# State space tables moved behind the modulation, its small operations moved to ScalarE, in the first stage of a two-block kernel

## The chip, the cores and the metric

One core of a Trainium2 chip. The metric is the device time of one execution in microseconds; the median of three runs stands for the kernel. Five engines work side by side: TensorE (PE, with its weight loads PEld), VectorE (DVE), ScalarE (ACT), GpSimd (POOL) and SyncE (SP), which issues most of the DMAs.

## The reference, cut to what matters

Two blocks are computed on 512 tokens of width 1024. Only the beginning of the first one matters here: the condition `c` gives shift, scale and gate through `w_ada`; the input is normed, scaled and shifted; then it is projected. Beside that, the state space mixer needs tables that hang on the weights alone: `lam_bar`, its powers, and `b_bar`.

```python
def first_block(x, c, ...):
    cond = jax.nn.silu(c)
    mod = cond @ w_ada[l] + b_ada[l]
    shift, scale, gate = jnp.split(mod, 3, axis=-1)
    h = rms_norm(x, norm_g[l]) * (1.0 + scale[:, None, :]) + shift[:, None, :]
    proj = h @ w_in[l]
    ssm_u, ssm_z, q, k, v, attn_z, q_idx, k_idx, w_idx = jnp.split(proj, split_points, axis=-1)
    y_ssm = s5_mixer(ssm_u, a_re[l], a_im[l], log_dt[l], b_re[l], b_im[l], ...)
    y_attn = dsa_mixer(q, k, v, q_idx, k_idx, w_idx, ...)
    ...

def s5_mixer(u, a_re, a_im, log_dt, b_re, b_im, ...):
    lam = lax.complex(a_re, a_im)
    dt = jnp.exp(log_dt)[:, None]
    lam_bar = jnp.exp(lam * dt)
    b_bar = ((lam_bar - 1.0) / lam)[..., None] * (b_re + i b_im)
    ...

def dsa_mixer(...):
    rel = jnp.einsum('bqhd,bsd->bqhs', qib, k_idx)       # the indexer
    score = jnp.einsum('bqh,bqhs->bqs', wib, jax.nn.relu(rel))
    _, sel = lax.top_k(score, topk)
    ...
```

## The kernel before, in words

The kernel holds the activations transposed: 8 tiles of 128 channels by 512 tokens. A product in full precision is made of three products of hi and lo parts (`mm3`, L152 to L155): `split` (L142 to L146) lets ScalarE round a tile to its hi part and VectorE or GpSimd subtract it to get the lo part.

**The modulation** (`block1`, from L448). For each tile k the rows of `w_ada` for shift and scale are loaded (`fetch`, L473) and multiplied with the condition `cB`. `weigh` (L486 to L492) does this on VectorE, where one instruction also sums (L490), or on GpSimd (L492), where ScalarE sums afterwards (`total`, L496). Shifts are weighed on VectorE, scales of the tiles 1 to 6 on GpSimd. `modulate(k, R)` (L498 to L504) then adds `b_ada` (L500) and forms (1 + scale) * norm_g (L501), both operations on one or two columns; L502 multiplies xT with it and with the row of inverse norms R, which lies in PSUM; L503 (ScalarE) adds the shift and rounds to the hi part hTh; L504 (VectorE) makes the lo part hTl. Of each tile `u_part(k)` takes 12 products for the state space input, and `i_part(k)` three for the indexer's keys. GpSimd makes the lo parts of their weights (`split_u`, `split_i`, L146).

**The tables** (`ssm_tables`, from L1106). This is a generator. Its first part, up to `yield None` (L1172), makes the exponential and sine and cosine of `lam * dt`, the powers of `lam_bar` (PW), and the factors kr and ki; nearly all are VectorE operations on 128 x 16 elements, one per `yield` (96 in all; the helpers are `poly_exp`, `sincos` with L1043 to L1057, `cmul` with L1065 and L1067). The second part makes Bb and the products BP (q 0 and 1 on VectorE, 2 and 3 on GpSimd), and then GpSimd makes the table of rotations `turn`, which starts from the phase and rho products L1194 to L1200.

In `block1` `step(n)` draws n steps of the first part. 40 are drawn at the beginning, 20 behind the making of the diagonal for R, and 8 after each `modulate(k)`, so that the first part is done after tile 4. Those 56 steps hold 59 VectorE instructions.

**The order of the work.** TensorE, SyncE and, in the first stage, ScalarE execute in the order of the program. The order on VectorE and GpSimd is fixed by the compiler's scheduler, by the order of the program and by what it takes to be ready; `tc.issue_after(x)` keeps the VectorE instructions of a block behind instruction x. All engines execute in the order that results.

**Behind it** the second part of the tables is drawn by `weave` (L230) together with the indexer's product:

```python
tables = later(tables)      # each step issued after `last`, the last hTl
self.weave(self.both(self.bias_table(), self.alongside(ssm_chunks(), tables)), indexer())
```

`weave` draws from `main` and lets each step's cost (the number that it yields, 0.12 for a small table operation, 0.62 for a product BP) buy steps of `indexer()`, 0.49 for three products of 384 columns. The indexer takes four column blocks; each ends with two evictions by `stack` (ScalarE L891, VectorE L892), out of two PSUM buffers. Its weights are loaded in four pieces and split by ScalarE (L145) and VectorE (L146). Then the scores (`index_scores`, L947 to L954) and the selection (`top_mask`, L965 to L974) follow, woven with the state space scan and with projections, and then attention.

Of the kernel before, what the change touches and what calls it, by code (L numbers as in the profile page):

```python
# [8 lines left out]
F32 = mybir.dt.float32  # L9
F32R = mybir.dt.float32r  # L10
I32 = mybir.dt.int32
AF = mybir.ActivationFunctionType
OP = mybir.AluOpType
# [91 lines left out]
class Kern:  # L105
# [342 lines left out]
    def block1(self):  # L448
        nc, A, tc = self.nc, self.A, self.tc
        sm = self.sm  # L450
        TT, TS, STT = nc.vector.tensor_tensor, nc.vector.tensor_scalar, nc.vector.scalar_tensor_tensor
# [16 lines left out]
        def fetch(k):  # L468
            wts[k] = []
            for v in range(2):  # L470
                tag = ("wlo", "whi")[v]
                wts[k].append(self.wp.tile([128, 1024], F32, name="wada", tag=tag, bufs=self.wbufs[tag]))
                nc.sync.dma_start(wts[k][v], wada[v * D + k * 128:v * D + (k + 1) * 128])  # L473
# [4 lines left out]
        def fetch_u(k):  # L478
            raw[k] = self.pg("uraw")
            nc.sync.dma_start(raw[k], A["w_in"][k * 128:(k + 1) * 128, 0:512])  # L480
            wu[k] = uhi[:, k], self.sp.tile([128, 512], F32R, name="ulo", tag=f"F{'ri'[k // 4]}{k % 4}", bufs=1)

        def split_u(k, eng):
            self.split(raw[k], *wu[k], eng=eng)

        def weigh(k, v, eng):  # L486

            w, m = wts[k][v], mod[:, 2 * k + v:2 * k + v + 1]
            if eng is nc.vector:
                eng.tensor_tensor_reduce(out=w, in0=w, in1=cB, scale=1.0, scalar=0.0, op0=OP.mult, op1=OP.add, accum_out=m)  # L490
            else:
                eng.tensor_tensor(out=w, in0=w, in1=cB, op=OP.mult)  # L492

        def total(k, v):
            w = wts[k][v]
            nc.scalar.activation(w, w, AF.Identity, accum_out=mod[:, 2 * k + v:2 * k + v + 1])  # L496

        def modulate(k, R):  # L498
            m = mod[:, 2 * k:2 * k + 2]
            TT(out=m, in0=m, in1=self.col("b_ada")[:, k:k + 9:8], op=OP.add)  # L500
            STT(out=m[:, 1:2], in0=m[:, 1:2], scalar=1.0, in1=self.col("norm_g", k), op0=OP.add, op1=OP.mult)  # L501
            STT(out=xT[k], in0=xT[k], scalar=m[:, 1:2], in1=R, op0=OP.mult, op1=OP.mult)  # L502
            nc.scalar.activation(hT[0][k], xT[k], AF.Identity, bias=m[:, 0:1])  # L503
            return STT(out=hT[1][k], in0=xT[k], scalar=m[:, 0:1], in1=hT[0][k], op0=OP.add, op1=OP.subtract)  # L504

        tables = self.ssm_tables()

        ready = []

        def step(n):  # L510
            while n and not ready:
                n -= 1
                if next(tables) is None:
                    ready.append(True)

        uacc = []

        def u_part(k):
            for j in range(4):
                if k == 0:  # L520
                    uacc.append(self.ps((128, 512), "ggss"[j]))
                self.mm3(uacc[j], [w[:, j * 128:(j + 1) * 128] for w in wu[k]], [v[k] for v in hT], k == 0, k == 7)
# [5 lines left out]
        def fetch_i():  # L528
            for h in range(2):
                iraw.append(self.pg("iraw").rearrange("p (k n) -> p k n", n=128)[:, :, :72])  # L530
                nc.sync.dma_start(iraw[h], A["w_in"][h * 512:(h + 1) * 512, 3584:3656].rearrange("(k p) n -> p k n", p=128))

        def split_i():
            for h in range(2):
                v = [self.pg("iw", F32R).rearrange("p (k n) -> p k n", n=128)[:, :, :72] for _ in range(2)]
                self.split(iraw[h], *v, eng=P)
                wk.extend([(v[0][:, k], v[1][:, k]) for k in range(4)])

        def i_part(k):
            self.mm3(kacc, wk[k], [v[k] for v in hT], k == 0, k == 7)  # L540

        with tc.manual_schedule(engines={mybir.EngineType.Activation}):
            V, P = nc.vector, nc.gpsimd
            for k in range(8):
                nc.sync.dma_start(xT[k], A["xT"][k * 128:(k + 1) * 128])
                if k == 7:
                    nc.sync.dma_start(cB, A["c_row"])
                self.square(xT[k], acc[k % 2], k // 2, (P if k % 2 else V) if k < 6 else (V if k == 7 else P))
            nc.scalar.activation(cB, cB, AF.Silu)
            step(40)  # L550
            for k in range(4):
                fetch(k)
                fetch_u(k)
                if k == 1:
                    fetch_i()
            warm = self.sm.tile([128, 1], F32, name="warm", tag="warm", bufs=1)
            nc.scalar.activation(warm, self.ones[:, 0:1], AF.Sqrt)
            TT(out=acc[0], in0=acc[0], in1=acc[1], op=OP.add)
            r = self.stats(acc[0])
            weigh(0, 0, V)  # L560
            weigh(0, 1, V)
            split_u(0, P)
            R = self.rows(r,'psum')
            with tc.issue_after(self.diag.ins):
                weigh(1, 0, V)
                step(20)
            weigh(1, 1, P)
            for k in range(8):
                last = modulate(k, R)
                with tc.issue_after(last.ins):  # L570
                    step(8)
                if 0 < k + 1 <= 6:
                    total(k + 1, 1)
                if k < 6:
                    weigh(k + 2, 1, P if k + 2 <= 6 else V)
                if k < 7:
                    split_u(k + 1, P)
                if k < 6:
                    weigh(k + 2, 0, V)
                if k == 0:  # L580
                    split_i()
                u_part(k)
                if k >= 0:
                    i_part(k - 0)
                if k < 4:
                    fetch(k + 4)
                    fetch_u(k + 4)
                    if k + 4 == 1:
                        fetch_i()
            for k in range(8, 8):  # L590
                i_part(k)
            with tc.issue_after(last.ins):
                step(1000)
            self.ssm_loads()
            self.ssm_inputs()
        self.dump("hT", hT[0])
# [17 lines left out]
        def later(stream):  # L614

            while True:
                with tc.issue_after(last.ins):
                    ask = next(stream, None)
                if ask is None:
                    return  # L620
                yield ask

        tables = later(tables)
# [482 lines left out]
    def ssm_tables(self):  # L1106
        nc, A, big = self.nc, self.A, self.sp
        TT, TS, STT = nc.vector.tensor_tensor, nc.vector.tensor_scalar, nc.vector.scalar_tensor_tensor
# [9 lines left out]
        def norm():  # L1118
            TT(out=den, in0=ar, in1=ar, op=OP.mult)
            yield 0.12  # L1120
            TT(out=t1, in0=ai, in1=ai, op=OP.mult)
            yield 0.12
            TT(out=den, in0=den, in1=t1, op=OP.add)
            yield 0.12
            nc.vector.reciprocal(den, den)
            yield 0.12

        dt, _ = yield from self.abreast(self.poly_exp(lam[:, 32:48], 16, "dt"), norm())
# [40 lines left out]
        yield from self.abreast(powers(PW, 7), coef())  # L1169
        self.PW = PW  # L1170

        yield None  # L1172
        B = self.Bm
        Bb = self.two("Bb")
        tb = self.two("tb") + self.two("tb")
# [32 lines left out]
        n = 1  # L1208
# [658 lines left out]
```

## Time and profile before

| | |
|---|---|
| median of three runs | 1264.85 us (1262.48 to 1265.42) |
| the profiled execution: time, span | 1264.23 us, 1262.2 us |
| mean granted TensorE clock | 0.973 |
| PE busy | 1161.3 us, 92% of the span |
| DVE busy | 823.2 us, 65% |
| ACT busy | 548.1 us, 43% |
| POOL busy | 450.0 us, 36% |

Times in the trace are counted from the start of the span. Busy time holds waiting too: an instruction that has started and waits for a port of the memory is shown as running. Small instructions overlap, so that several of 0.17 us can start 0.08 us apart. A wait in brackets is idle time of the engine before an instruction, with what ended it.

### The profile page before, as it was taken

The numbers are of one execution on the slowest core, as the hardware profiler recorded it, in microseconds if no ns is written. First come the engines' busy times: TensorE is split into PE (matmuls) and PEld (weight loads), VectorE is DVE, ScalarE is ACT, GpSimd is POOL, SyncE is SP. The second block draws the span as 40 slices with busy tenths as digits, with TensorE's granted clock in tenths as the row PEclk, the third lists the DMA queues.
The fourth block names the chain that finished last, engine by engine and source line by source line (L and its number), as shares of the span: only waits on it lengthen the run. The fifth ranks groups of instructions, "written<-read, shape, count | busy, mean of one in ns | idle before, by whom it ended". The sixth has DMA issues, their size and how long they took to land.

```text
span 1262.2 us, 17119 instructions
## 1 busy us (share of the span) xinstructions
PE 1161.3 (92%) x6264; PEld 949.0 (75%) x6264; DVE 823.2 (65%) x1602; ACT 548.1 (43%) x1022; POOL 450.0 (36%) x546
## 2 busy tenths in 40 slices
PE   2667888977899999898999999999999999999998
PEld 2457787965678998886777777688888888888876
DVE  7986999438765466786767575564577743577731
ACT  4333532145663543555565555433444421344420
POOL 4679689048532037245666565201000000000000
PEclk9797988988999999999999999999999999999999
DMA  9452113145134442232111111134333233333330
GB/s 355 140 151 69 35 54 103 34 151 166 34 103 159 149 121 61 68 101 67 35 34 51 34 34 35 50 100 150 101 94 90 90 98 96 100 92 92 98 111 34
DMA packets 112755, 118.05 MB, mean 94 GB/s; under 512 B 16184, under 2 KB 101216, under 8 KB 112672
## 3 DMA queue, kind: packets, MB, share of 16 engines
q1 hardware_dynamic: 102432, 107.20, 26.9%
q10 hardware_dynamic: 10240, 9.77, 2.4%
q8 instruction: 49, 0.80, 0.3%
q14 instruction: 34, 0.28, 0.1%
HBM read 109.47 MB, written 6.30 MB: 92 GB/s over the span
## 4 chain that ended last, share of the span: by engine, by line
PE 76%; DVE 17%; ACT 2%; issue 2%; DMA 1%; POOL 1%; ACTq 0%; DVEq 0%; POOLq 0%
PE ps_g L153 20%; PE ps_g L154 20%; PE ps_g L155 19%; PE ps_t L369 4%; PE ps_o L383 4%; DVE wlo L146 2%; PE ps_s L342 2%; PE ps_s L341 2%; DVE score L954 1%; PE ps_t L1321 1%; DVE score L971 1%; DVE wada L490 1%; DVE m L970 1%; PE ps_o L1659 1%; PE ps_t L1325 1%
## 5 line engine op out<-in xcount | busy, mean ns | idle before, releaser
L145 ACT CAST whi<-wraw 128x1024 fp32r<-128x1024 f32 (+4 forms) x161 | 161.8, 1011 | 170.1 <-PE ps_g L154 136.6
L146 DVE TENSOR_TENSOR wlo<-wraw,whi 128x1024 fp32r<-128x1024 f32 (+4 forms) x143 | 174.8, 1228 | 69.4 <-ACT whi L145 69.3
L153 PE MATMUL ps_g<-hT,whi 128*128 128x512 f32 x504 | 206.6, 410 | 0.0
L155 PE MATMUL ps_g<-hT,wlo 128*128 128x512 f32 x504 | 197.9, 393 | 0.0
L154 PE MATMUL ps_g<-hT,whi 128*128 128x512 f32 x504 | 196.3, 390 | 0.0
L350 POOL TENSOR_TENSOR P<-P,rsum 128x256 f32<-128x256 f32 (+3 forms) x144 | 100.4, 727 | 76.2 <-DVE rsum L1446 34.3
L345 ACT ACTIVATE P<-P,nm 128x128 f32<-128x128 f32 (+3 forms) x160 | 89.7, 561 | 85.4 <-DVE nm L343 84.7
L153 PEld LDWEIGHTS ps_g<-hT,whi 128*128 128x128 f32 x504 | 95.1, 189 | 24.4 <-issue 9.3
L155 PEld LDWEIGHTS ps_g<-hT,wlo 128*128 128x128 f32 x504 | 94.7, 188 | 21.9
L154 PEld LDWEIGHTS ps_g<-hT,whi 128*128 128x128 f32 x504 | 95.0, 189 | 17.9 <-issue 1.2
L343 DVE CUSTOM_DVE_ANT_0 P<-ps_s,att 128x128 f32<-128x128 f32 (+3 forms) x128 | 62.1, 485 | 50.6 <-PE ps_t L369 29.4
L369 PE MATMUL ps_t<-consts,P 128*128 128x128 f32 x400 | 66.3, 279 | 11.4 <-DVE qst L895 7.5
L153 PE MATMUL ps_g<-act,whi 128*128 128x512 f32 (+1 forms) x176 | 70.8, 403 | 0.0
L155 PE MATMUL ps_g<-act,wlo 128*128 128x512 f32 (+1 forms) x176 | 68.8, 391 | 0.0
L154 PE MATMUL ps_g<-act,whi 128*128 128x512 f32 (+1 forms) x176 | 68.8, 391 | 0.0
L153 PE MATMUL ps_g<-whi,hTh 128*128 128x256 f32 x192 | 61.2, 319 | 7.0 <-ACT sq L666 4.3
L369 PEld LDWEIGHTS ps_t<-consts,P 128*128 128x128 f32 x400 | 46.7, 141 | 26.9 <-issue 14.7
L855 POOL TENSOR_TENSOR acc<-acc,sq 128x512 f32<-128x512 f32 x15 | 21.9, 1461 | 117.9 <-ACT sq L854 115.2
L153 PE MATMUL ps_g<-whi,hT 128*128 128x256 f32 (+1 forms) x208 | 59.0, 284 | 2.8 <-ACT sq L1361 2.8
L154 PE MATMUL ps_g<-wlo,hT 128*128 128x256 f32 (+1 forms) x208 | 58.5, 281 | 2.4 <-DVE wlo L146 2.4
L155 PE MATMUL ps_g<-whi,hT 128*128 128x256 f32 (+1 forms) x208 | 58.4, 281 | 0.0
L154 PE MATMUL ps_g<-wlo,hTh 128*128 128x256 f32 x192 | 56.4, 294 | 0.9 <-DVE wlo L146 0.9
(508 smaller groups left out, 2915.8 us busy)
## 6 DMA issues: line engine op xcount, KB each, us to landing
wraw<-in_w_in_dram SPq DMA_DIRECT2D x56, 512.0 KB, 3.4
wraw<-in_w_up_dram SPq DMA_DIRECT2D x40, 512.0 KB, 3.7
wada<-in_w_ada_dram SPq DMA_DIRECT2D x16, 512.0 KB, 7.2
wraw<-in_w_down_dram SPq DMA_DIRECT2D x16, 512.0 KB, 3.4
wadag<-in_w_ada_dram SPq DMA_DIRECT2D x8, 512.0 KB, 4.5
wraw<-in_w_out_dram SPq DMA_DIRECT2D x8, 512.0 KB, 3.3
wraw<-in_w_attn_br_dram SPq DMA_DIRECT2D x8, 512.0 KB, 3.4
wraw<-in_w_o_dram SPq DMA_DIRECT2D x8, 512.0 KB, 3.4
```

Source lines behind the costliest of these rows:

```text
L145: nc.scalar.copy(hi, src)
L146: (eng or nc.vector).tensor_tensor(out=lo, in0=src, in1=hi, op=OP.subtract)
L153: mm(out, lhsT=l[0], rhs=r[0], start=start, stop=False)
L154: mm(out, lhsT=l[0], rhs=r[1], start=False, stop=False)
L155: mm(out, lhsT=l[1], rhs=r[0], start=False, stop=stop)
L341: nc.tensor.matmul(s, lhsT=q, rhs=khi[:, :w], start=True, stop=False)
L342: nc.tensor.matmul(s, lhsT=q, rhs=klo[:, :w], start=False, stop=True)
L343: nc.vector.tensor_tensor_reduce(out=P[i], in0=s, in1=madd(i), scale=-1.0, scalar=3.0e38, op0=OP.add, op1=OP.min, accum_out=nm[:, i:i + 1])
L345: nc.scalar.activation(P[i], P[i], AF.Exp, scale=-1.0, bias=nm[:, i:i + 1], accum_out=sums[:, i:i + 1])
L350: nc.gpsimd.tensor_tensor(out=P[n], in0=P[n], in1=sc[:, n:n + 1].to_broadcast([128, (n + 1) * 128]), op=OP.mult)
L369: nc.tensor.transpose(pt[:, o:o + 128], P[i][:, j * 128:(j + 1) * 128], self.ident)
L383: nc.tensor.matmul(acc[x * 64:(x + 1) * 64, j * 128:], lhsT=V(j), rhs=tiles[b][:, o:o + w], start=start and j == 0, stop=stop and j == 2)
```

## The change

The first part of the tables is no longer drawn between the modulations. The 40 steps at the beginning stay; the rest is drawn by the weave with the indexer's product, where the second part already stands, and so behind the last hTl. The `yield None` that parted the two is gone. In `modulate` the two small VectorE operations become two ScalarE operations: the shift gets its bias by an Identity with a column of `b_ada` as bias, and the scale by one with `norm_g` as scale and a column of the new table `one` = (b_ada + 1) * norm_g as bias, which one VectorE operation makes at the start for all eight tiles.

```diff
         def modulate(k, R):
             m = mod[:, 2 * k:2 * k + 2]
-            TT(out=m, in0=m, in1=self.col("b_ada")[:, k:k + 9:8], op=OP.add)
-            STT(out=m[:, 1:2], in0=m[:, 1:2], scalar=1.0, in1=self.col("norm_g", k), op0=OP.add, op1=OP.mult)
+            nc.scalar.activation(m[:, 0:1], m[:, 0:1], AF.Identity, bias=self.col("b_ada", k))
+            nc.scalar.activation(m[:, 1:2], m[:, 1:2], AF.Identity, scale=self.col("norm_g", k), bias=one[:, k:k + 1])
             STT(out=xT[k], in0=xT[k], scalar=m[:, 1:2], in1=R, op0=OP.mult, op1=OP.mult)
...
+        one = self.cp.tile([128, 8], F32, name="one")
+        STT(out=one, in0=self.col("b_ada")[:, 8:16], scalar=1.0, in1=self.col("norm_g"), op0=OP.add, op1=OP.mult)
         tables = self.ssm_tables()
 
-        ready = []
-
         def step(n):
-            while n and not ready:
-                n -= 1
-                if next(tables) is None:
-                    ready.append(True)
+            for _ in range(n):
+                next(tables)
...
             with tc.issue_after(self.diag.ins):
                 weigh(1, 0, V)
-                step(20)
             weigh(1, 1, P)
             for k in range(8):
                 last = modulate(k, R)
-                with tc.issue_after(last.ins):
-                    step(8)
                 if 0 < k + 1 <= 6:
                     total(k + 1, 1)
...
-            with tc.issue_after(last.ins):
-                step(1000)
             self.ssm_loads()
             self.ssm_inputs()
...
         yield from self.abreast(powers(PW, 7), coef())
         self.PW = PW
 
-        yield None
         B = self.Bm
```

## Rows read from the trace of the kernel before

**Rows 1.** Busy time by stretch: stretch and its length, then each engine, clock, DMA.
```profile
24.65:69.91 45.26, 31.87 (x101) 21.88 (x100) 44.47 (x106) 16.15 (x29) 29.01 (x34) 0.85 0.44 152
69.91:109.70 39.79, 25.50 (x128) 22.44 (x126) 30.08 (x33) 12.48 (x23) 32.10 (x54) 0.87 0.40 120
109.70:185.00 75.30, 64.79 (x557) 61.66 (x558) 66.03 (x116) 33.26 (x67) 59.24 (x64) 0.87 0.18 57
185.00:1262.20 1077.20, 1035.72 (x5469) 839.61 (x5468) 664.58 (x1285) 475.36 (x889) 321.42 (x386) 0.99 0.28 87
```

**Rows 2.** Waits from 15 to 76 us: who waits for whom, total, times, longest.
```profile
ACT hTh L503 <- DVE xT L502: 34.0, 7, 7.8
```

**Rows 3.** Timeline, 0 to 40 us: start, duration, engine, line, operation, tiles.
```profile
34.06 3.75 DVE L1055 SCALAR_TENSOR_TENSOR trc<-trc,tr 128x16 f32<-128x16 f32 x3
34.17 2.34 POOL L492 TENSOR_TENSOR wada<-wada,cB 128x1024 f32<-128x1024 f32 x1
...
36.52 1.26 POOL L146 TENSOR_TENSOR ulo<-uraw,uhi 128x512 fp32r<-128x512 f32 x1
```

**Rows 4.** The tile mod, 0 to 70 us: shortest, median and longest in ns.
```profile
L500 DVE TENSOR_TENSOR mod<-mod,vecs x8: 146/178/1246, 18.8 to 65.6; 128x2 f32<-128x2 f32 x8
L501 DVE SCALAR_TENSOR_TENSOR mod<-mod,vecs x8: 145/156/2261, 19.9 to 65.8; 128x1 f32<-128x1 f32 x8
```

**Rows 5.** Chain of waits, 0 to 180 us: start, the time it takes there, what.
```profile
57.07 1.14 DVE wada L490
58.21 0.67 DVE hTl L504
```

**Rows 6.** Timeline: first tile's modulation, and hTh of tile 6.
```profile
24.65 0.17 DVE L1000 SCALAR_TENSOR_TENSOR erq<-erq,err 128x16 f32<-128x16 f32 x1
...
25.38 0.74 DVE L502 SCALAR_TENSOR_TENSOR xT<-xT,mod,ps_t 128x512 f32<-128x512 f32 x1
...
26.15 0.72 ACT L503 ACTIVATE hTh<-xT,mod 128x512 fp32r<-128x512 f32 x1 [7.76 <-DVE xT L502]
...
66.70 0.72 ACT L503 ACTIVATE hTh<-xT,mod 128x512 fp32r<-128x512 f32 x1 [2.82 <-DVE xT L502]
```

**Rows 7.** GpSimd's groups, 18.7 to 69.9 us: busy us, mean ns, idle before.
```profile
L146 POOL TENSOR_TENSOR iw<-iraw,iw 128x288 fp32r<-128x288 f32 x2 | 1.6, 794 | 0.0
...
L1195 POOL TENSOR_TENSOR kt<-trs 128x16 f32<-128x16 f32 x1 | 0.2, 211 | 0.0
```

**Rows 8.** Timeline, 0 to 40 us, ScalarE.
```profile
17.68 0.21 ACT L278 ACTIVATE rt<-ms 128x4 f32<-128x4 f32 x1 [3.36 <-DVE ms L277]
...
34.80 1.04 ACT L496 ACTIVATE wada<-wada 128x1024 f32<-128x1024 f32 x1
...
35.84 0.60 ACT L145 CAST uhi<-uraw 128x512 fp32r<-128x512 f32 x1
```

**Rows 9.** Timeline, 68 to 130 us, VectorE.
```profile
68.59 1.32 DVE L504 SCALAR_TENSOR_TENSOR hTl<-xT,mod,hTh 128x512 fp32r<-128x512 f32 x1 [0.38 <-ACT hTh L503]
...
75.11 1.73 DVE L146 TENSOR_TENSOR wlo<-wraw,whi 128x1024 fp32r<-128x1024 f32 x1 [4.68 <-ACT whi L145]
...
83.51 0.68 DVE L1065 TENSOR_TENSOR t<-kpwr,Bb 128x512 f32<-128x512 f32 x1
...
92.07 0.55 DVE L892 TENSOR_TENSOR iq<-ps_g,iq 64x384 fp32r<-64x384 f32 x1
...
109.13 0.56 DVE L892 TENSOR_TENSOR iq<-ps_g,iq 64x384 fp32r<-64x384 f32 x1 [0.54 <-ACT iq L891]
```

**Rows 10.** Timeline, 68 to 190 us, GpSimd and TensorE.
```profile
70.24 1.79 POOL L1103 COPY CD<-ssm 64x256 f32<-64x256 f32 x4
...
97.46 0.66 PE L153 MATMUL ps_g<-hTh,whi 128*128 128x384 f32 x1 [11.97 <-DVE iq L892]
...
142.80 1.28 POOL L1288 TENSOR_TENSOR rot<-turn,E 128x512 f32<-128x512 f32 x1 [8.44 <-issue]
```

**Rows 11.** VectorE's groups, 18.7 to 69.9 us: busy us, mean ns, idle before.
```profile
L1055 DVE SCALAR_TENSOR_TENSOR trc<-trc,tr 128x16 f32<-128x16 f32 x7 | 6.6, 937 | 0.1
```

## The prediction, made before the change was run

> **What bounds the kernel now.** The change touches the first 110 us, so I read the trace there in stretches, from the engines' busy shares down to single instructions. The busy table by stretch [rows 1] shows four regimes. In the first stage (24.65 to 69.91, modulation and first products) VectorE is busy 44.47 of 45.26 us and TensorE 31.87. In the second (to 109.70, the indexer's product beside the state space tables) no engine is full, yet something is always waited for. In the third (to 185) VectorE is busy 66.03 of 75.30. Behind 185 TensorE is busy 96% and the work is fixed. So the end of the kernel moves by as much as the first two stages give, if the third passes it on.
>
> The waits of the first stage [rows 2] name one thing: ScalarE's hi cast of a tile (hTh, L503) waits seven times, 34.0 us together, for VectorE's scaling of xT (L502). What holds VectorE is seen in the timeline [rows 3]: three operations on 16 elements (L1055) take 3.75 us, and end when GpSimd's weighing product (34.17 to 36.51) and lo part (36.52 to 37.78) end. An operation with two inputs in SBUF waits out GpSimd's instruction; L502, with its second input in PSUM, never does. The two small modulation operations (L500, L501) take 0.15 us alone and up to 1.25 and 2.26 [rows 4]. So the full VectorE is mostly a VectorE that waits for GpSimd, and the stage is bound by what the two may not do at once.
>
> **The sum.** Per tile that exclusive work is GpSimd's lo part 1.26 and weighing 2.34 [rows 3], VectorE's weighing 1.14 and hTl 0.67 [rows 5]: 5.4 us. Measured from the hTh of tile 0 to that of tile 6 [rows 6] it is (66.70 - 26.15) / 6 = 6.76. The rest is what the change takes away:
> - Tables: 59 VectorE instructions leave the stage. Free, they start 0.08 apart (24.65 to 25.38 holds nine of them) [rows 6], I take 0.088: 5.2 us. With them go 18 small GpSimd products on their results (phase and rho, L1194 to L1200), 0.21 each [rows 7]: 3.8.
> - Modulation: 16 small VectorE operations, 0.15 each [rows 4]: 2.4.
>
> That is 11.4 us of exclusive time, but not all is path. Worked forward: L502 of tile 0 starts 0.73 sooner, hTh(0) at 25.4. Tile 0 to 1 takes 5.4 plus the two lo parts of the indexer's weights (1.6 [rows 7]), four tiles 5.4, tile 5 to 6 only 4.2 (both weighings on VectorE, 1.26 + 2 x 1.14 + 0.67): hTh(6) at 58.2. Its own 0.72, then the cast 0.60, two small ScalarE operations 0.6, L502, hTh and hTl of tile 7 (0.74, 0.72, 0.67) are 4.1: the last hTl ends at 62.3 in place of 69.91 (68.59 + 1.32) [rows 9]. **Term 1: -7.6.**
>
> On ScalarE the new chain of a tile is L502 0.74, hTh 0.72 [rows 6], the sum of the weighed product 1.04, the cast 0.60 and two new one-column operations [rows 8]. The trace has none; the nearest are 0.21 (four columns) [rows 8] and 0.72 (512 columns with a bias) [rows 6]. I take 0.3 each, near the first: 3.7 a tile, under the 5.4 that cover it. If that cover went, each costs its 0.3; by the upper bound the chain would be 4.5, still under. The trace speaks for ScalarE being free: it waits 34.0 us [rows 2]. The Trainium skill, page ScalarE: Activation LUTs, section Rules for kernel authors, says the contrary of the edit: adds and multiplies go to VectorE. With its 0.28 and 0.37 us for one and two pointer operands (an estimate from What ACT_TABLE_LOAD costs) against 0.30 on VectorE it would cost 8 x 0.35 = 2.8 us, a time of 1260, were ScalarE the bound; no run here shows that yet. The one new table operation (`one`, 8 columns) needs only the vectors loaded first and runs ahead of the stage: nothing, 0.17 (a small operation [rows 6]) if VectorE has no gap there.
>
> The tables come back behind the last hTl. VectorE's first weight split there starts 5.2 us after it, of which 4.68 is idle, waiting for ScalarE [rows 9]. In the new kernel 5.2 us of table operations plus GpSimd's copies for CD, 1.79 us [rows 10], which hold the same port, want that place: 7.0 against 5.2. What is late next is that weight split, and TensorE behind it. **Term 2: +1.8.** The 18 GpSimd products fall into GpSimd's own waits (for the tables, then for Bb), so nothing for them; uncovered, 3.8. The DMA queues are not moved: no transfer hangs on a table, and the weights of the modulation are fetched when their buffers come free, sooner than now.
>
> Then the indexer. Its first eviction (iq, 92.07) stands on VectorE behind table products that begin at 83.51 [rows 9] (five of them), 1.6 us each beside GpSimd, and TensorE idles 11.97 us for it [rows 10]. In the new weave the 59 small operations pay for indexer columns first, so the products begin later against TensorE; I count one product fewer in front. **Term 3: -1.5**, bounds 0 and -8.
>
> Sum -7.3. The profiled execution took 1264.23 (span 1262.2 and 2.0 around it), 0.6 below the median shown; so 1256.9 to 1257.6: **1257.5**. The third stage passes it on: VectorE's scores and selection fill it [rows 1] and start when iq is done.
>
> **Rivals.**
> - *TensorE's idle goes too.* If the compiled order puts the first evictions ahead of the products, the 11.97 us shrink. For: the new weave charges the small operations against the indexer. Against: the order on VectorE is decided by what is ready, and the small ones are ready in the idle 4.68 us, which leaves the products where they are. GpSimd's rotation has 8.44 us of slack [rows 10], so hardly more than 8 can be had: -7.6 + 1.8 - 8 = -13.8, 1250.7.
> - *The port is the only limit.* Then all 11.4 us count: -11.4 + 1.8 - 1.5 = -11.1, 1253.4. For: VectorE's 44.47 of 45.26 [rows 1]. Against: GpSimd is busy only 29.01 there, and waits for casts. The Trainium skill, SBUF page (SBUF — State Buffer), section SBUF: two separate sides, states this as a rule, a lock held for the whole instruction by whoever starts first. The trace agrees where the three small operations ended with GpSimd's.
> - *It comes back whole.* Nothing hides the tables but the idle 4.68: +5.2 + 3.8 - 4.7 = +4.3, no relief of the indexer: -3.3, 1261.3, no change that can be told. For: the same instructions, the same port.
> - *Slower.* The tables pay in the new place what they paid in the old: seven at 0.94 [rows 11], 52 at 0.17 without overlap, 15.4, and GpSimd's 3.8 between them, all ahead of the first weight split: 15.4 + 3.8 - 4.7 = +14.5, less 7.6: +6.9, 1271.4. It decides when that split starts over 12.8 us (7.6 + 5.2) behind the last hTl. For: GpSimd's small products use the results while the rest still runs. Against: GpSimd has no 2 us instruction in that place.
>
> **How the numbers follow.** Forecast 0.40; TensorE's idle goes 0.22; port alone 0.10; comes back 0.17; slower 0.11. A measurement of this kernel tells about 0.3%, 3.8 us, from no change: faster means under 1261.1. The forecast's own range is 1254 to 1259.1 (Term 3 at -5 and at 0). Faster: the first three less 0.02 (Term 1 too small), 0.70. Same: 0.18. Slower: 0.12, with 0.01 for the bad end of the fourth. The range runs from 1249.5, which leaves out some 0.07 beyond the first rival, to 1264.5, which leaves out the slower cases.
>
> **What would show it.** Right: hTh of tile 0 to tile 6 in about 33 us instead of 40.6; the last hTl near 62.3; no L500 or L501 on VectorE, 16 ScalarE operations of about 0.3; the first weight split 6 to 8 us behind the last hTl; the last iq near 102 instead of 109.13 [rows 9]. Wrong: a tile pitch still over 6.3 (then ScalarE or the buffers bound it); the first split 10 us or more behind the last hTl; or an iq that is earlier while the selection in the third stage is not.

## The result, and the profile after

The changed kernel takes 1255.28 us (median, 1254.63 to 1258.95) beside 1265.42 for the kernel before in the same session: ratio 0.9924, 95% interval 0.9906 to 0.9941, or 7.5 to 11.9 us. Every ratio below is to the kernel before, run in the same session, with its 95% interval in brackets. The profiled spans are 1253.5 and 1262.2, so 8.7 us are there to be found. 1257.5 was forecast, and the range held the result.

**The first stage.** Timeline of the changed kernel, ScalarE (the hTh of tile 0 and tile 6, and between them the two moved operations of tile 6) and VectorE (the L502 that waits for them):

```profile
26.10 0.72 ACT L503 ACTIVATE hTh<-xT,mod 128x512 fp32r<-128x512 f32 x1 [6.75 <-DVE xT L502]
...
57.90 0.29 ACT L500 ACTIVATE mod<-mod,vecs 128x1 f32<-128x1 f32 x1
58.10 0.37 ACT L501 ACTIVATE mod<-mod,one,vecs 128x1 f32<-128x1 f32 x1
58.51 0.75 DVE L502 SCALAR_TENSOR_TENSOR xT<-xT,mod,ps_t 128x512 f32<-128x512 f32 x1 [1.00 <-ACT mod L501]
59.29 0.72 ACT L503 ACTIVATE hTh<-xT,mod 128x512 fp32r<-128x512 f32 x1 [0.82 <-DVE xT L502]
```

From tile 0 to tile 6 it is 33.2 us, where it was 40.6 [rows 6]. The busy table by stretch (columns as in [rows 1]) shows that VectorE is no longer full:

```profile
24.65:62.00 37.35, 28.39 (x98) 19.86 (x98) 29.84 (x31) 19.15 (x43) 27.38 (x15) 0.91 0.52 189
```

**The second stage.** Timeline of the changed kernel, VectorE; the rows answer to those of [rows 9]:

```profile
62.57 0.75 DVE L504 SCALAR_TENSOR_TENSOR hTl<-xT,mod,hTh 128x512 fp32r<-128x512 f32 x1 [0.80 <-ACT hTh L503]
...
71.76 2.34 DVE L146 TENSOR_TENSOR wlo<-wraw,whi 128x1024 fp32r<-128x1024 f32 x2
...
79.27 0.55 DVE L886 TENSOR_TENSOR iq<-ps_g,iq 64x384 fp32r<-64x384 f32 x1 [3.17 <-ACT iq L885]
...
109.27 0.56 DVE L886 TENSOR_TENSOR iq<-ps_g,iq 64x384 fp32r<-64x384 f32 x1
```

The last hTl ends at 63.3 instead of 69.9. The tables run behind it, from 63.3 to 71.2. The first weight split starts 8.4 us behind the last hTl instead of 5.2. The first iq is 12.8 us earlier than before, but the last one stands where it stood.

TensorE, changed kernel, behind the indexer's matmuls, which are done at 91.8 (107.5 before):

```profile
100.05 0.55 PE L153 MATMUL ps_g<-whi,hTh 128*128 128x256 f32 x1 [8.04 <-DVE iq L886]
104.59 0.58 PE L154 MATMUL ps_g<-wlo,hTh 128*128 128x256 f32 x1 [3.99 <-DVE wlo L146]
```

The 11.97 us of waiting for VectorE, which stood inside the indexer's product [rows 10], now stand behind it, as 8.04 + 3.99. What counts is the second row: from there TensorE runs on with the projections. The same matmul in the kernel before:

```profile
111.77 0.58 PE L154 MATMUL ps_g<-wlo,hTh 128*128 128x256 f32 x1 [0.89 <-DVE wlo L146]
```

So 7.2 us are gained at this point, 7.1 behind the first scores (121.09 against 128.22), 7.9 at the last instruction of the selection (227.8 against 235.7) and 8.7 at the end.

**The points of the path.** The traces of the runs below at the same points (us from the start of the span; "cast" is ScalarE's first whi behind the last hTl, "split" VectorE's first wlo, "resumes" TensorE's first L154 of 256 columns, "scores" VectorE's addition of `consts` to the first finished scores; in brackets the distance from the point to its left):

| kernel | last hTl ends | cast | split | resumes | scores |
|---|---|---|---|---|---|
| before | 69.9 | 74.0 (4.1) | 75.1 (1.1) | 111.8 (36.7) | 128.2 (16.4) |
| changed | 63.3 | 70.1 (6.8) | 71.8 (1.7) | 104.6 (32.8) | 121.1 (16.5) |
| tables alone | 66.3 | 70.4 (4.1) | 73.9 (3.5) | 106.8 (33.0) | 121.4 (14.5) |
| tables alone, second execution | 66.4 | 70.5 (4.2) | 74.0 (3.5) | 107.0 (33.0) | 121.6 (14.6) |
| modulation alone | 67.2 | 74.3 (7.1) | 75.4 (1.1) | 113.8 (38.4) | 127.7 (13.9) |
| order alone | 70.0 | 74.1 (4.1) | 75.2 (1.1) | 107.7 (32.4) | 124.0 (16.3) |
| modulation and order | 67.8 | 75.0 (7.1) | 76.1 (1.1) | 107.8 (31.7) | 122.4 (14.7) |
| changed, old order | 63.6 | 70.4 (6.8) | 72.2 (1.8) | 109.4 (37.2) | 123.6 (14.2) |
| changed, tables thrice, unpaid | 63.4 | 70.2 (6.8) | 72.4 (2.3) | 105.9 (33.4) | 120.5 (14.6) |
| scales weighed on VectorE | 57.4 | 62.8 (5.4) | 65.2 (2.4) | 98.9 (33.6) | 113.5 (14.7) |
| all port work on VectorE | 56.5 | 62.0 (5.5) | 64.3 (2.3) | 98.3 (34.0) | 112.9 (14.6) |
| products on VectorE | 63.2 | 70.0 (6.8) | 71.7 (1.7) | 96.1 (24.4) | 118.6 (22.5) |
| scales and products on VectorE | 57.4 | 62.8 (5.4) | 65.2 (2.4) | 90.2 (25.0) | 114.9 (24.7) |

Each row is one execution; the two of the same kernel differ by 0.1 to 0.2 us at these points.

### The profile page after: what moved, and what is told of

Same layout as the page of the kernel before. It is cut to its first block, busy times and chain, and to the rows that moved or that the text cites. A ratio compares the mean times of both kernels' runs of the same rounds, so it can differ in the third digit from the quotient of the medians.

```text
span 1253.5 us, 17119 instructions
## 1 busy us (share of the span) xinstructions
PE 1159.3 (92%) x6264; PEld 949.0 (76%) x6264; DVE 815.6 (65%) x1587; ACT 552.8 (44%) x1038; POOL 459.5 (37%) x546
## 4 chain that ended last, share of the span: by engine, by line
PE 76%; DVE 15%; ACT 3%; POOL 2%; issue 2%; DMA 1%; SPq 0%; ACTq 0%; DVEq 0%; POOLq 0%
PE ps_g L153 20%; PE ps_g L154 20%; PE ps_g L155 19%; PE ps_t L369 4%; PE ps_o L383 4%; DVE wlo L146 2%; PE ps_s L342 2%; PE ps_s L341 2%; DVE wada L490 1%; PE ps_t L1314 1%; DVE score L965 1%; DVE score L948 1%; PE ps_o L1652 1%; DVE t L1059 1%; PE ps_t L1318 1%
## 5 line engine op out<-in xcount | busy, mean ns | idle before, releaser
L154 PE MATMUL ps_g<-hT,whi 128*128 128x512 f32 x504 | 198.1, 393 | 0.0
L154 PEld LDWEIGHTS ps_g<-hT,whi 128*128 128x128 f32 x504 | 95.3, 189 | 18.8 <-issue 1.2
L153 PE MATMUL ps_g<-act,whi 128*128 128x512 f32 (+1 forms) x176 | 70.2, 399 | 0.0
L154 PE MATMUL ps_g<-act,whi 128*128 128x512 f32 (+1 forms) x176 | 69.1, 393 | 0.0
L154 PE MATMUL ps_g<-wlo,hT 128*128 128x256 f32 (+1 forms) x208 | 58.7, 282 | 2.4 <-DVE wlo L146 2.4
L154 PE MATMUL ps_g<-wlo,hTh 128*128 128x256 f32 x192 | 56.3, 293 | 4.0 <-DVE wlo L146 4.0
```

The lines of the kernel that those rows point to most:

```text
L153: mm(out, lhsT=l[0], rhs=r[0], start=start, stop=False)
L154: mm(out, lhsT=l[0], rhs=r[1], start=False, stop=False)
```

## The experiments

**One part at a time.** In the first run the tables move and the two modulation operations stay on VectorE; in the second the tables stay.

```diff
 # tables alone: the changed kernel, but
-            nc.scalar.activation(m[:, 0:1], m[:, 0:1], AF.Identity, bias=...)
-            nc.scalar.activation(m[:, 1:2], m[:, 1:2], AF.Identity, scale=..., bias=...)
+            TT(out=m, in0=m, in1=self.col("b_ada")[:, k:k + 9:8], op=OP.add)
+            STT(out=m[:, 1:2], in0=m[:, 1:2], scalar=1.0, in1=self.col("norm_g", k), ...)
 # modulation alone: the kernel before with the opposite edit
```

> The tables move behind the last hTl; the two small modulation operations stay on VectorE. Theory (the port that VectorE's two-input operations and GpSimd share sets the pace): 9.0 of the 11.4 us of exclusive time leave the stage, the 2.4 of the modulation stay; hTh of tile 0 to tile 6 in about 35 us (33.2 with the whole change, 40.6 before), time about 1257.5. Rival (the small modulation operations matter most, because they stand between the sum and L502, and each waits for a GpSimd product): most of the gain is missing, hTh 0 to 6 over 38 us, time 1261 to 1264.

> Only the small modulation operations move to ScalarE; the tables stay between the modulations. Theory of the port: 2.4 us of exclusive time leave, hTh 0 to 6 about 38.5 us, time about 1263. Rival (the modulation operations matter most): hTh 0 to 6 under 36 us, time 1257 to 1259. Third (ScalarE's operations cost the chain of a tile): no gain or slower, 1265 to 1268.

Tables alone: 1256.12, ratio 0.9934 [0.9919, 0.9948]. Modulation alone: 1265.47, ratio 1.0006 [0.9995, 1.0018]. In the first stage the two add up: hTh of tile 0 to 6 takes 36.7 and 37.0 us, 3.9 and 3.6 less than 40.6, and 7.4 less with both. At the end they don't: the tables bring 8 us with 3.7 of them in the first stage (the theory's 1257.5, nearly), and the modulation brings nothing with its 2.7, though it shortens the stage by more than its theory had.

Where the 2.7 go is seen on ScalarE. Timelines, first the kernel before, then modulation alone:

```profile
73.55 0.59 ACT L604 COPY Y<-ps_g 128x512 f32<-128x512 f32 x1 [0.46 <-PE ps_g L155]
...
74.03 1.05 ACT L145 CAST whi<-wraw 128x1024 fp32r<-128x1024 f32 x1
...
74.98 1.07 ACT L604 COPY Y<-ps_s 128x512 f32<-128x512 f32 x2
```

```profile
73.81 0.59 ACT L606 COPY Y<-ps_s 128x512 f32<-128x512 f32 x1 [0.65 <-PE ps_o L155]
74.29 1.05 ACT L145 CAST whi<-wraw 128x1024 fp32r<-128x1024 f32 x1
```

Before, the cast stood behind two of the four copies of Y, which wait for TensorE's last products; with the two small operations on ScalarE it stands behind all four. So it starts at 74.3, where it was at 74.0, although the last hTl ends 2.7 sooner, and VectorE's first split waits 7.74 us for it instead of 4.68. In the changed kernel the cast is behind the four copies too, and behind two operations more, the first of which waits for TensorE:

```profile
66.81 1.12 ACT L598 COPY Y<-ps_s 128x512 f32<-128x512 f32 x2
69.22 0.47 ACT L913 COPY R<-ps_s 8x384 f32<-8x384 f32 x1 [1.28 <-PE ps_s L912]
69.59 0.57 ACT L625 CAST kk<-ps_o 64x512 fp32r<-64x512 f32 x1
70.07 1.99 ACT L145 CAST whi<-wraw 128x1024 fp32r<-128x1024 f32 x2
```

Why the scheduler chooses these orders isn't shown.

**The order alone.** The tables' 56 late steps bring their cost into the weave, and this buys columns of the indexer's product ahead of the products BP. The cost isn't 56 x 0.12 = 6.72, as this run and its expectation take it: 18 of the steps, those of the powers by `cmul`, yield 0.15 and not 0.12, so it is 7.26. The run is 0.54 short of it, about one step of the indexer (0.49). One call gives the kernel before nearly the same order (three iq ahead of the first product, as in the changed kernel) and moves nothing:

```diff
-        self.weave(self.both(self.bias_table(), self.alongside(ssm_chunks(), tables)), indexer())
+        self.weave(self.both(self.bias_table(), self.alongside(ssm_chunks(), self.both(self.hold(6.72), tables))), indexer())
```

> The kernel before, in which only the weave is told a cost of 6.72 (56 steps of 0.12) ahead of the second part of the tables: columns of the indexer's product are then placed ahead of the products BP as in the changed kernel, while the tables stay in the first stage and the modulation on VectorE. The run with the tables alone gained 3.7 us to the last hTl and 8.1 at the end. Theory (the rest of some 4.4 us comes from the order in which evictions and products stand): the last hTl where it was (69.9), the end earlier by 3 to 5 us, 1260 to 1262. Rival (it comes from the tables themselves being gone from the first stage, by the weights and copies that are ready sooner): no change, 1264 to 1266. A second rival (the indexer's evictions then displace the products and the state space path becomes late): slower by 1 to 3.

1259.71, ratio 0.9960 [0.9945, 0.9975]: 0.3 below the theory's range, and neither rival's. Timeline of this run, TensorE:

```profile
105.83 0.55 PE L153 MATMUL ps_g<-whi,hTh 128*128 128x256 f32 x1 [7.87 <-DVE iq L892]
107.66 0.58 PE L154 MATMUL ps_g<-wlo,hTh 128*128 128x256 f32 x1 [1.28 <-DVE wlo L146]
```

The split is where it was (75.2), and TensorE resumes 4.1 us sooner. About half of the change's gain is had without moving one operation.

**The order taken away.** The changed kernel, with the 56 late steps at no cost:

```diff
+        def unpaid(steps):
+            for n, cost in enumerate(steps):
+                yield 0.0 if n < 56 else cost
-        self.weave(... self.alongside(ssm_chunks(), tables)), indexer())
+        self.weave(... self.alongside(ssm_chunks(), unpaid(tables))), indexer())
```

> The changed kernel, in which the 56 table steps cost nothing in the weave, so that products BP and the indexer's columns stand to each other as in the kernel before; the tables stay in their late place and the modulation's two operations on ScalarE. Theory (the gain is made of three terms: the last hTl 6.6 sooner, some 4.1 from the order, as the run of the order alone gave, and the late tables costing 3.5): without the order's term TensorE resumes behind the indexer at 108 to 109 instead of 104.6, time 1259 to 1260.5. Rival (the order matters only where the tables are gone from the late place; here the small operations delay the products anyway): within 1 of 1255.3.

1259.85, ratio 0.9958 [0.9944, 0.9973]: the theory's time. TensorE, same row as above, 0.4 later than the theory had it:

```profile
109.43 0.58 PE L154 MATMUL ps_g<-wlo,hTh 128*128 128x256 f32 x1 [0.89 <-DVE wlo L146]
```

4.8 us later than in the changed kernel, and by the ratios (0.9958 - 0.9924) x 1264.3 = 4.3 more in the time. The two runs give the order's share from both sides: 4.1 and 4.8 us at TensorE, and by the ratios 5.1 and 4.3 in the times, each give or take 2 to 3. The section on the clock comes back to the second.

**The modulation with the order.**

```diff
 # the kernel before with both edits: modulation on ScalarE, hold(6.72) ahead of the tables
```

> The kernel before with the modulation's two operations on ScalarE and the weave's cost of 6.72 ahead of the second part of the tables; the tables stay in the first stage. The modulation alone gave 2.7 us to the last hTl and nothing at the end; the order alone gave 4.6 at the end. Theory (the modulation's gain was lost to the old order, which put more products ahead of the first eviction): both add, 2 to 3 us below the order alone, 1256.5 to 1258. Rival (the gain is lost at the first weight split, which waits for ScalarE until 75.2 whatever the last hTl does): as the order alone, 1259 to 1260.5.

1259.62, ratio 0.9955 [0.9939, 0.9972]: the rival. It resumes at 107.8 as the order alone does (107.7): the last hTl is 2.2 us sooner, but the split is 0.8 later (76.1), since the cast stands behind four copies again:

```profile
74.97 1.05 ACT L145 CAST whi<-wraw 128x1024 fp32r<-128x1024 f32 x1
```

**The tables three times.** Are the late tables on the path? First with their cost in the weave, then without:

```diff
-        yield from self.abreast(powers(PW, 7), coef())
+        for _ in range(3):
+            yield from self.abreast(powers(PW, 7), coef())
 # unpaid: once as it was, then
+        for _ in range(2):
+            for _ in self.abreast(powers(PW, 7), coef()):
+                yield 0.0
```

> The changed kernel, in which the powers and the factors kr and ki are computed three times in their late place: 54 more VectorE operations on 128 x 16 elements, which at 0.09 us each are 5 us more of table work ahead of the first weight split of the second stage. Nothing else is added. Theory (the tables stand on the path there: the first weight split waits behind them and TensorE behind the split): +4 to +6, 1259 to 1261, and the first weight split some 13 us behind the last hTl instead of 8.4. Rival (VectorE has slack in the second stage, and the tables are hidden by the wait of TensorE for iq): at most +1, 1255 to 1256.5.

> The changed kernel, in which the powers and the factors kr and ki are computed three times in their late place as before, but the added steps cost nothing in the weave, so that they buy no columns of the indexer's product and the order of evictions and products stays that of the changed kernel (the earlier run of this kind lost 15 us, most of it since all eight evictions came ahead of the products). 54 more small VectorE operations, 0.09 us each: 4.9 us. Theory (tables in the late place are on the path to TensorE's resumption behind the indexer): resumption at 104.6 + 4 to 5 us, 1259 to 1261. Rival (hidden in VectorE's waits for ScalarE and for evictions): at most +1, under 1256.5.

The first gave 1270.34, ratio 1.0036 [1.0020, 1.0053], by the ratios 14 us more than the changed kernel, which neither theory had: the added cost (54 steps or 7.56 on top of 7.26) bought all eight evictions ahead of the products, and TensorE stopped for these instead. Its timeline, TensorE:

```profile
103.42 0.47 PE L1249 MATMUL ps_t<-consts,BPr 128*128 128x128 f32 x1 [7.85 <-DVE BPr L1061]
...
111.27 0.47 PE L1249 MATMUL ps_t<-consts,BPi 128*128 128x128 f32 x1 [7.11 <-DVE BPi L1061]
```

So a higher price is not better still: of the three that were run with late tables (0, 7.26 and 14.82), the middle one is the best. The second run, with the order of the changed kernel but for one iq, gave 1256.27, ratio 0.9928 [0.9906, 0.9949]: by the ratios 0.5 above the changed kernel, inside both intervals. 54 more operations move the first split by 0.67 us (from 71.76), not by 4.9:

```profile
72.43 1.21 DVE L146 TENSOR_TENSOR wlo<-wraw,whi 128x1024 fp32r<-128x1024 f32 x1
```

TensorE resumes 1.3 us later (105.9). So 54 operations beside the 59 that are late, 4.9 us of them, cost about a microsecond there: the late tables are hidden for the most part.

**Less port work in the first stage.** All scales are weighed on VectorE, so that GpSimd's 2.34 us instruction and ScalarE's sum leave the tile loop; then the lo parts of the state space weights too.

```diff
-            weigh(1, 1, P)
+            weigh(1, 1, V)
-                if 0 < k + 1 <= 6:
-                    total(k + 1, 1)
-                    weigh(k + 2, 1, P if k + 2 <= 6 else V)
+                    weigh(k + 2, 1, V)
 # second run, in addition
-            split_u(0, P)
+            split_u(0, V)
-                    split_u(k + 1, P)
+                    split_u(k + 1, V)
```

> The whole change, and the weighings of the scales of tiles 1 to 6 go from GpSimd (2.34 us each, and a sum of 1.23 on ScalarE) to VectorE (1.14 with the sum). Theory of the port: exclusive time per tile falls from 5.4 to 1.26 + 2 x 1.14 + 0.67 = 4.2; hTh 0 to 6 in about 26 us instead of 33.2, time about 1249. Rival (VectorE's own load sets the pace): VectorE gets six more instructions, 6.8 us, hTh 0 to 6 in 36 to 40 us, time 1258 to 1262.

> The run with all scales weighed on VectorE, and in addition the lo parts of the state space weights (two of 128 x 512 a tile are one of 1.26 us on GpSimd) on VectorE too, so that GpSimd has none of the port's turns in the tile loop. VectorE's work per tile is then two weighings of 1.14, the scaling 0.74, hTl 0.67 and a lo part of about 0.67: 4.4 us, against a measured distance of 4.7 between tiles with GpSimd's 1.26 in it. Theory (the port alone bounds the stage: exclusive work falls from 2 x 1.14 + 0.67 + 1.26 = 4.2 to VectorE's own 4.4): hTh of tile 0 to 6 in 26 to 28 us against 28.5, 1247 to 1249. Rival (the fetch of the rows of the modulation's weights or ScalarE bounds it now): tile distance unchanged at 4.7, time within 0.5 of 1248.9. Second rival (VectorE's lo part holds up the next weighing): distance over 5, 1251.

The first gave 1248.92, ratio 0.9877 [0.9863, 0.9890]: faster than both kernels, and the time of the theory of the port (1249). Tile 0 to 6 takes 28.5 us, where that theory had 26 and the rival 36 to 40. Its timeline, VectorE and GpSimd, one tile:

```profile
34.43 1.21 DVE L490 CUSTOM_DVE_ANT_0 wada<-wada,cB 128x1024 f32<-128x1024 f32 x1
...
35.57 0.74 DVE L504 SCALAR_TENSOR_TENSOR hTl<-xT,mod,hTh 128x512 fp32r<-128x512 f32 x1
35.85 1.61 POOL L146 TENSOR_TENSOR ulo<-uraw,uhi 128x512 fp32r<-128x512 f32 x1 [3.10 <-ACT uhi L145]
36.24 2.30 DVE L490 CUSTOM_DVE_ANT_0 wada<-wada,cB 128x1024 f32<-128x1024 f32 x1
38.47 0.08 DVE L490 DVE_READ_ACCUMULATOR2_ANT mod<- 128x1 f32 x1
38.47 0.74 DVE L502 SCALAR_TENSOR_TENSOR xT<-xT,mod,ps_t 128x512 f32<-128x512 f32 x1
```

One weighing takes 1.21 us; the other, which meets GpSimd's lo part (1.26 us alone), 2.30. In the changed kernel, with GpSimd's weighing beside them, single ones take up to 3.42. The second run gave 1249.05, ratio 0.9871 [0.9846, 0.9897]: tiles in the middle are now 4.2 us apart instead of 4.7 (hTh at 35.30 and 39.52), tile 0 to 6 takes 27.4, within the theory's 26 to 28, the last hTl is 0.9 sooner, and the time is the same: neither a gain nor a loss can be told.

**The other products on VectorE.** BP of q 2 and 3 move from GpSimd, first in the changed kernel, then beside the scales weighed on VectorE.

```diff
-            yield from self.cmul(nc.vector if q < 2 else nc.gpsimd, ..., 0.62 if q < 2 else 0.0)
+            yield from self.cmul(nc.vector, ..., 0.62)
```

> The whole change, and the products BP of q 2 and 3 go from GpSimd to VectorE (12 instructions more on VectorE, alone 0.67 each; GpSimd's twelve took 1.2 to 1.6 each, in turns with VectorE's). Theory of the port: the stretch of the products, 22 us now (84.6 to 106.2), becomes 24 x 0.67 = 16; TensorE resumes behind the indexer about 5 us sooner, time about 1250. Rival (VectorE's load in the second stage sets the pace): 12 x 0.67 = 8 us more on VectorE, TensorE resumes 5 to 8 us later, time 1260 to 1263.

> The run with all scales weighed on VectorE, and in addition the products BP of q 2 and 3 on VectorE instead of GpSimd. Alone on the changed kernel, the second edit let TensorE resume 8 us sooner and was worth 0 to 1.4 us at the end. Theory (the third stage is bound by VectorE's total work, so that TensorE's idle in the second stage is worth nothing): the same as without it, 1248 to 1249.5. Rival (with the first stage shorter, the products end soon enough for the third stage to take over what TensorE gains): 3 to 6 us less, 1243 to 1246.

1257.06, ratio 0.9938 [0.9925, 0.9951], and 1251.83, ratio 0.9893 [0.9867, 0.9920]. The first is neither the theory's time nor the rival's, the second above both. TensorE resumes 8.5 us sooner (96.1 and 90.2), and nothing of it is left: it then stops for ScalarE's relu. That stands in ScalarE's order behind a copy of We, which waits 7.50 us (7.63 in the second run) for a product on VectorE. TensorE and ScalarE in the first run, then TensorE in the second:

```profile
108.94 0.59 ACT L1251 COPY We<-ps_t 128x512 f32<-128x512 f32 x1 [7.50 <-DVE t L1059]
...
110.11 0.58 PE L941 MATMUL ps_s<-kk,iq 128*128 128x256 f32 x1 [4.22 <-ACT relu L944]
```

```profile
104.24 0.58 PE L939 MATMUL ps_s<-kk,iq 128*128 128x256 f32 x1 [3.98 <-ACT relu L942]
```

That VectorE's work bounds the third stage fits, but what is shown is this one wait for its products; 8.5 us at TensorE were worth nothing.

**The clock.** The modulation's part is worth 2.2 us where TensorE resumes (106.8 with the tables alone, 104.6 in the changed kernel) and 0.3 at the scores. The granted clock shows where most of the rest goes. TensorE by stretch (length, busy, clock, DMA), first the changed kernel, then the tables alone:

```profile
107.00:110.00 3.00, 3.00 (x18) 0.50 0.39 108
110.00:112.00 2.00, 2.00 (x11) 0.50 0.94 279
112.00:114.00 2.00, 2.00 (x13) 0.50 0.99 323
114.00:116.00 2.00, 2.00 (x19) 0.97 0.27 96
```

```profile
107.00:110.00 3.00, 3.00 (x16) 0.53 0.59 175
110.00:112.00 2.00, 1.16 (x13) 1.00 0.24 45
```

Here 0.50 is the lower of the two levels, 1.2 GHz, and 1.00 is 2.4 GHz. Behind two idle stretches of nearly the same length (8.0 and 4.0 us, 8.1 and 4.0) the changed kernel stays at 1.2 GHz for 9.5 us (104.6 to 114.1, worked out from 0.97 in the last row), the other for 3.0 (106.8 to 109.8, from 0.53). The kernel before has the long stretch too, 111.8 to 121.2. The last run asked whether this is the kernel's or the execution's; its kernel is that of the tables alone.

> The kernel with the tables alone moved, once more, to see whether the stretch at TensorE's lower granted clock behind the indexer is a property of the kernel or of the execution. In its first profile that stretch lasted 2.9 us from 106.84 on, in the changed kernel 9.8 us from 104.59 on, behind the same two idle stretches of 8 and 4 us. Theory (it falls out anew in each execution): a length that differs from 2.9 by over 1 us. Rival (it is fixed by what TensorE did before): 2.9 again, within 0.5. Time 1254 to 1258 in both.

The clock rises at 110.7, 3.7 us behind the resumption at 107.0, and the time of this one execution is 1257.09. That is a difference of 0.7, outside the rival's 0.5 and under the theory's 1, so neither holds as it was put; it is near the first length and far from 9.5. With two executions it looks like the kernel's own; what decides it stays open. In the table the distance from resumption to scores is 16.3 to 16.5 with a long stretch (9.2 to 9.5 us: before, changed, order alone) and 13.9 to 14.7 with a short one (2.8 to 4.0: the others, but for the two with products on VectorE): about 2 us.

This touches two readings above. The changed kernel with the old order and the one with the tables thrice, unpaid, have the short stretch, so at the scores the first is 2.5 us behind the changed kernel instead of 4.8, and the second 0.6 ahead of it. Order alone and before both have the long one: 4.1 us at the resumption, 4.2 at the scores. But those 2 us aren't seen at the end: order alone (long) and modulation with order (short) lie 1.6 us apart at the scores, and 0.1 in their times.

## Why the prediction was right, and where its steps were wrong

- **Term 1 (-7.6)** held in sum: 33.2 us where 33 was said, the last hTl at 63.3 where 62.3 was said, -6.6. Tile by tile it did not: 4.2, 9.0, 6.2, 3.9, 6.3 and 3.6 us, where 7.0, four times 5.4 and 4.2 were said, so that it fits so closely is in part luck. The runs with one part add up to it, and moving GpSimd's weighing to VectorE shortened the stage again, by 4.7 us from tile 0 to 6. So the stage was bound mostly by what VectorE and GpSimd may not do at once. The rival that the port is the only limit (-11.4) fell: VectorE now idles 5.5 us for hTh and 2.0 for L501.
- **The ScalarE pair** took 0.29 and 0.37 us, against 0.3 each. The page ScalarE: Activation LUTs of the Trainium skill gives, in What ACT_TABLE_LOAD costs, 0.28 us with one pointer operand and 0.093 more for another, so 0.37 (an estimate), and the trace agrees. That 5.4 us a tile "cover" them did not hold everywhere: L502 waits for L501 at the tiles 1, 6 and 7, 2.0 us together, while ScalarE waits 20.3 for L502 over the stage. The same page of the Trainium skill, in Rules for kernel authors, sends adds and multiplies to VectorE, for their time per element. On ScalarE the two cost at most those 2.0 us of VectorE's time in this stage, and the stage was still 3.6 us shorter with this edit alone. What the prediction missed is behind the stage: the cast of the weights was ordered 2.6 to 3.0 us later, which took back the edit's gain where it stood alone.
- **Term 2 (+1.8)** measured +3.2, and its cause was wrong. I named the table operations; of the 3.2 us, 2.6 are ScalarE's cast, which stands behind four copies of Y and two operations more, and 0.6 the tables. Where the cast is early (tables alone), the tables do cost 2.4. That VectorE would fill its wait with them is right: 54 more operations moved the split by 0.67 us and TensorE's resumption by 1.3.
- **Term 3 (-1.5)** measured -3.8 in the changed kernel and was the term most mis-sized. The mechanism was the one named: the small operations pay for indexer columns first. But it is worth 4.3 to 5.1 us in the time, shown by adding it alone and by taking it away. I counted "one product fewer in front" of the first iq; in fact the first three iq come ahead of all products. My argument that the products stay "where they are" because the idle 4.68 us take the small operations was wrong: the idle decides when these run, the price decides what stands ahead of what.
- **The sum** (-7.3) came out as -7.2 at TensorE's resumption because the errors of Terms 2 and 3, +1.4 and -2.3, nearly cancel with Term 1's +1.0. That the sum is right is luck to this extent. The 1.6 us that come behind the scores (8.7 - 7.1) have no run of their own and stay unexplained; executions of the changed kernel differ by more (1254.63 to 1258.95).
- **The sign "last iq near 102" failed**: it is at 109.27. The first evictions come 13 us sooner, the last ones wait for the products. The step "start when iq is done" is wrong with it: the scores are finished 7.1 us sooner with the last iq unmoved, as TensorE's resumption is 7.2 sooner.
- **TensorE's idle goes too** (1250.7) fell: 12.0 us are idle for VectorE as before, only behind the indexer. Where most of that was taken away (products on VectorE), nothing came of it. **It comes back whole** fell with the relief of the indexer, 3.8 us where it said none, and **slower** with the first split at 8.4 us, under the 12.8 from which it decides.

## What to carry to other kernels

A block that moves into a planned stream brings its price with it. Here the price of 56 small steps changed the order of evictions and products, and that was worth about as much as taking the steps out of the full stage (4.1 to 4.8 us at TensorE, against 3.7 at the last hTl); try the price alone first. A gain in one stage has to be followed to the instruction that opens the next (here a cast on ScalarE, then TensorE's resumption): 2.7 us vanished at the one and 8.5 behind the other, and a table of the same few points over the runs showed where.

## What the hardware showed that was not expected

Two idle stretches of nearly the same length (8.0 and 4.0 us) were followed by 9.5 us at the lower clock in one kernel and by 3.0 and 3.7 in two executions of another, which is some 2 us at the scores, where the whole change moved 7.1. And a VectorE weighing that takes 1.21 us took 3.42 beside GpSimd's weighing; the eight of the first stage average 2.03 us in the changed kernel's trace.
